# One level of Strassen's scheme in the gate and up product of an encoder's MLP

## The chip, the cores and the metric

The kernel runs on one core of one Trainium2 chip. The metric is the device time of one execution in microseconds (us). The engines that matter are TensorE (PE in the rows; its weight loads are listed as PEld), VectorE (DVE), ScalarE (ACT), GpSimd (POOL), and SyncE (SP), whose queue issues nearly all DMA transfers.

## The reference

Two encoder layers run over 1024 tokens of width 1024. Each has a mixer (attention of one kind or the other), a cross-attention into 256 memory tokens, and a gated MLP; every one is followed by a residual sum with the factor alpha and a LayerNorm. The change is in the MLP:

```python
def conv_ffn(x, w_in, conv_w, conv_b, w_out):
    g, u = jnp.split(x @ w_in, 2, axis=-1)          # 1024 -> 2 x 2816
    g = causal_depthwise_conv(g, conv_w, conv_b)    # width 3, along the tokens
    h = jax.nn.gelu(g.astype(f32)) * u.astype(f32)
    return h.astype(x.dtype) @ w_out                # 2816 -> 1024
```

All values are float32.

## The kernel before, in words

Every float32 operand of a product is split in two: a rounded part `hi` (a cast on ScalarE) and a rest `lo` (a subtraction on VectorE); `split` does both. A product is then three matmuls, hi·hi, hi·lo and lo·hi, summed in PSUM. Weights come by DMA into one of two staging buffers `st`, are split into two buffers of an arena `R` of 20 (8 `rb` that live throughout, 12 `rx` that live from the end of a mixer to the end of the MLP), and are fetched in a fixed order (`weights`, `w_emit`, `w_take`), two ahead. PSUM has eight banks of 128x512: four tiles `s1` of one bank and two tiles `d2` of two.

The normalised input of the MLP lies token-major in `acc` (eight tiles of 128 tokens by 1024). `to_xT` transposes a tile on TensorE (eight 128x128 transposes) and splits it into `xh` and `xl`, feature-major, eight K-blocks of 128 features by 1024 tokens.

The MLP's hidden width 2816 is cut into 22 blocks j of 128. `ffn_hidden` makes one block: the gate product and the up product, each 128 hidden units by 1024 tokens, as two halves of 512 tokens; a half is 8 K-blocks by 3 matmuls of 128x512 in `gemm_fm` (lines 144 to 146). VectorE and ScalarE then do the convolution (lines 379 to 382), the gelu (384), the product with the up branch (385) and the split of h. After each two blocks (four at the end) `ffn` multiplies h by the output weights, 8 token tiles by 2 halves by 3 matmuls for each block (lines 311 to 313), and VectorE adds the result onto `acc` (199, 201). The last group of blocks is followed tile by tile by the LayerNorm (`ln`, lines 171 to 181).

`mem` is the cross-attention, head by head (h = 0 to 3). In its last head the eight token tiles pass in turn through scores (`score`), a transpose of the weights (`tr`) and the product with the values (`pv`); the sum onto `acc` and LayerNorm follow, and `to_xT` transposes tile t-4 behind tile t. The last tiles' transposes are queued in `xtq` and done inside the first `ffn_hidden`.

The order of the work on each engine is laid out ahead of time by a scheduler that follows the program's order and fills in what is ready; on the chip each engine takes its list in order.

## Time and profile before

| what | us |
|---|---|
| median of 3 runs | 2884.42 |
| lowest and highest of them | 2881.32, 2886.17 |
| the profiled execution, its own time | 2884.2 |
| span of the profiled execution, first to last instruction | 2882.5 |
| mean granted TensorE clock in it | 0.998 |

The page gives busy time by engine and by line, and the windows, the timeline and the groups by form are answers of the same trace. A matmul's duration runs from when it enters the array to when its last column has left, and the next one enters before that; so the distance of two starts, not the duration, is what one more matmul adds. Waits are put down to the releaser that came last.

### The profile page before, as it was taken

To read this page: it belongs to the slowest core of one execution; us is meant where nothing else is said; L and a number is where in the kernel's file an instruction comes from. 1 tells how busy PE (TensorE), PEld (TensorE's weight loads), DVE (VectorE), ACT (ScalarE), POOL (GpSimd) and SP (SyncE) were. 2 spreads that over 40 slices of the span, in tenths; PEclk is the share of its full clock that TensorE was granted. 3 is DMA by queue.
4 is the path that set the end of the run, shared out by engine and by line. 5 is a ranking of instruction groups with operands and counts; after the bars stand their busy time and mean duration, and the time that the engine had idled before them with its cause. 6 is when DMAs were issued, how large, how long until landed. Compare 5 with 4: busy or idle time off the path is not lost.

```text
span 2882.5 us, 37533 instructions
## 1 busy us (share of the span) xinstructions
PE 2839.5 (99%) x15080; PEld 2391.4 (83%) x15080; DVE 1612.4 (56%) x2846; ACT 951.8 (33%) x1859; POOL 103.7 (4%) x155
## 2 busy tenths in 40 slices
PE   8999999999999999999999999999999999999998
PEld 7878888899988888888888777799988888888887
DVE  4647664855674444444448786665584444444446
ACT  4335463533342222222123565343343221122121
POOL 0000000100010000000001000100010000000001
PEclk9999999999999999999999999999999999999999
DMA  3113322422201111111123322332201111111111
GB/s 134 36 49 96 88 66 81 154 74 74 74 15 59 52 52 51 49 47 52 37 61 121 110 58 85 109 103 75 74 30 59 52 49 47 45 44 59 37 59 66
DMA packets 64512, 193.09 MB, mean 67 GB/s; under 512 B 11697, under 2 KB 11986, under 8 KB 64338
## 3 DMA queue, kind: packets, MB, share of 16 engines
q1 hardware_dynamic: 62976, 188.88, 21.3%
q8 instruction: 119, 1.95, 0.3%
q10 hardware_dynamic: 1362, 1.81, 0.2%
q14 instruction: 55, 0.45, 0.0%
HBM read 158.14 MB, written 9.44 MB: 58 GB/s over the span
## 4 chain that ended last, share of the span: by engine, by line
PE 75%; DVE 3%; DMA 1%; ACT 1%; issue 1%; POOL 1%; SPq 0%; DVEq 0%; ACTq 0%; POOLq 0%
PE s L145 12%; PE s L146 12%; PE s L144 12%; PE d L311 5%; PE d L313 5%; PE d L312 5%; PE s L246 2%; PE s L495 2%; PE s L497 2%; PE s L496 2%; PE d L526 2%; PE d L528 2%; PE d L527 2%; PE s L430 1%; PE s L432 1%; PE s L431 1%
## 5 line engine op out<-in xcount | busy, mean ns | idle before, releaser
L144 PE MATMUL s<-xh,rb 128*128 128x512 f32 x1824 | 714.2, 392 | 3.2 <-ACT xh L111 1.7
L145 PE MATMUL s<-xl,rb 128*128 128x512 f32 x1824 | 710.9, 390 | 0.6 <-DVE xl L112 0.6
L146 PE MATMUL s<-xh,rb 128*128 128x512 f32 x1824 | 710.5, 390 | 0.0
L112 DVE TENSOR_TENSOR rb<-st,rb 128x1024 fp32r<-128x1024 f32 (+1 forms) x207 | 252.1, 1219 | 285.9 <-ACT rb L111 278.9
L144 PEld LDWEIGHTS s<-xh,rb 128*128 128x128 f32 x1824 | 342.6, 188 | 74.1 <-ACT xh L111 2.2
L146 PEld LDWEIGHTS s<-xh,rb 128*128 128x128 f32 x1824 | 342.5, 188 | 71.2
L145 PEld LDWEIGHTS s<-xl,rb 128*128 128x128 f32 x1824 | 342.8, 188 | 69.8 <-DVE xl L112 1.5
L111 ACT CAST rb<-st 128x1024 fp32r<-128x1024 f32 (+1 forms) x207 | 217.1, 1049 | 433.3 <-PE s L145 275.2
L199 DVE TENSOR_TENSOR acc<-acc,d 128x1024 f32<-128x1024 f32 x160 | 195.3, 1221 | 198.0 <-PE d L313 167.9
L313 PE MATMUL d<-rx,rx 128*128 128x512 f32 x572 | 222.5, 389 | 0.0
L312 PE MATMUL d<-rx,rx 128*128 128x512 f32 x572 | 222.5, 389 | 0.0
L311 PE MATMUL d<-rx,rx 128*128 128x512 f32 x572 | 222.5, 389 | 0.0
L385 DVE TENSOR_TENSOR fc<-fc,s 128x512 f32<-128x512 f32 x88 | 60.5, 687 | 201.8 <-PE s L146 201.8
L111 ACT CAST rx<-st 128x1024 fp32r<-128x1024 f32 x40 | 40.5, 1051 | 339.3 <-PE d L312 321.6
L495 PE MATMUL s<-rx,xh 128*128 128x256 f32 x512 | 144.6, 282 | 0.0
L497 PE MATMUL s<-rx,xl 128*128 128x256 f32 x512 | 143.5, 280 | 0.0
L496 PE MATMUL s<-rx,xh 128*128 128x256 f32 x512 | 143.4, 280 | 0.0
L384 ACT ACTIVATE fc<-fc,cw 128x512 f32<-128x512 f32 x88 | 63.7, 724 | 225.8 <-DVE fc L382 225.8
L246 PE MATMUL s<-xh,rb 128*128 128x512 f32 x448 | 128.1, 397 | 3.7 <-ACT xh L111 1.0
L312 PEld LDWEIGHTS d<-rx,rx 128*128 128x128 f32 x572 | 107.4, 188 | 22.7
L311 PEld LDWEIGHTS d<-rx,rx 128*128 128x128 f32 x572 | 107.4, 188 | 22.3
L313 PEld LDWEIGHTS d<-rx,rx 128*128 128x128 f32 x572 | 107.4, 188 | 22.2
(300 smaller groups left out, 4952.5 us busy)
## 6 DMA issues: line engine op xcount, KB each, us to landing
st<-in_ffn_in_dram SPq DMA_DIRECT2D x88, 512.0 KB, 3.7
st<-in_ffn_out_dram SPq DMA_DIRECT2D x44, 512.0 KB, 3.6
st<-in_mem_kv_dram SPq DMA_DIRECT2D x32, 512.0 KB, 4.1
st<-in_memT_dram SPq DMA_DIRECT2D x16, 512.0 KB, 3.7
st<-in_mem_qT_dram SPq DMA_DIRECT2D x16, 512.0 KB, 3.6
st<-in_mem_out_dram SPq DMA_DIRECT2D x16, 512.0 KB, 3.6
Q<-rr SPq DMA_DIRECT2D x128, 64.0 KB, 2.0
st<-in_e_v_dram SPq DMA_DIRECT2D x8, 512.0 KB, 4.2
```

The costliest lines, as they stand in the source:

```text
L111: s.nc.scalar.copy(out=hi, in_=src)
L112: s.nc.vector.tensor_tensor(out=lo, in0=src, in1=hi.bitcast(F32), op=ALU.subtract)
L144: nc.tensor.matmul(ps, h[:, k, :], s.xh[:, k, t0:t1], start=k == 0, stop=False)
L145: nc.tensor.matmul(ps, h[:, k, :], s.xl[:, k, t0:t1], start=False, stop=False)
L146: nc.tensor.matmul(ps, l[:, k, :], s.xh[:, k, t0:t1], start=False, stop=k == NK - 1)
L199: s.nc.vector.tensor_tensor(out=a, in0=a, in1=ps, op=ALU.add)
L311: nc.tensor.matmul(o, hh[:, sl], wh[:, c], start=q == 0, stop=False)
L312: nc.tensor.matmul(o, hh[:, sl], wl[:, c], start=False, stop=False)
L313: nc.tensor.matmul(o, hl[:, sl], wh[:, c], start=False, stop=q == n - 1)
L495: nc.tensor.matmul(o, s.xh[:, k, sl], gh, start=k == 0, stop=False)
L496: nc.tensor.matmul(o, s.xh[:, k, sl], gl, start=False, stop=False)
L497: nc.tensor.matmul(o, s.xl[:, k, sl], gh, start=False, stop=k == NK - 1)
```

## The change

The gate and up product of block j is taken as a 2x2 by 2x2 block product: A11 and A12 are the gate weights for the first and second four K-blocks, A21 and A22 those of the up branch; B11, B12 are the first four K-blocks of x for the first and the last 512 tokens, B21 and B22 the second four. It is done with seven block products (Winograd's form of Strassen's scheme) in place of eight, each of four K-blocks by three matmuls of 128x512. The sums of weights S1 to S4 are made on VectorE for each j (`prep`) and split; the sums of inputs T1 to T4 are made once for each layer (`pair`, which takes token tiles t and t+4 together) and split. The first four tiles go to B11 and B21 as they come (`early`). Products that share a sum accumulate in one PSUM bank; the others are combined on VectorE (`post`). `early` and `pair` replace `to_xT` before the MLP; four products of blocks 0 and 1 that need only B11 and B21 stand between the pairs.

h is written to DRAM (`hid`), and the output product is a phase of its own: for each half of the tokens (g) and each j, h and the output weights are read back and split (`out_prep`), and four token tiles accumulate in all eight PSUM banks over the 22 blocks. `acc` serves as scratch in the meantime; x is kept in DRAM (`xres`). `mem`'s matrix G gets four buffers of its own (`GU`), and the arena keeps 16. The MLP's weights leave the list of `weights`; the next mixer's first weight is held back until the MLP's end (`hold`). The scratch that the program sets aside for DMA descriptors goes from 2048 to 1024. Lines that are left out of the diff below are pools, views and names.

```diff
+        s.hold = False
+        s.xres = s.dr.tile([T, D], F32, name="xres")
+        s.hid = [s.dr.tile([P, T], F32, name=f"hid{j}") for j in range(s.FF)]
...
-            if key[0] in ("eo", "oo") or (len(s.R.base) if key[0] in ("ok", "ov", "oa", "ob") else s.R.n()) < 2:
+            if key[0] in ("eo", "oo") or s.hold and key[0] == "ok" or (len(s.R.base) if key[0] in ("ok", "ov", "oa", "ob") else s.R.n()) < 2:
...
+        s.GU = [p.tile([P, Arena.W], F32R, name=f"gu{i}") for i in range(4)]
+        s.tmp = [p.tile([P, 512], F32, name=f"tmp{i}") for i in range(2)]
+        s.F = [p.tile([P, T + 8 + 104 * (i == 2)], F32, name=f"f{i}")[:, 0:T + 8] for i in range(3)]
+        s.open_x()
...
+    def open_x(s, more=()):
+        s.xs = ExitStack()
+        p = s.xs.enter_context(s.tc.tile_pool(name="restx", bufs=1, reuse_waits="tile"))
+        s.R.open([p.tile([P, Arena.W], F32R, name=f"rx{i}") for i in range(8)] + list(more))
+    def close_x(s):
+        s.R.close()
+        s.xs.close()
...
+    PRODS = {"P1": ("A11", "B11", 0), "P2": ("A12", "B21", 0), "P3": ("S4", "B22", 2), "P4": ("A22", "T4", 3),
+             "P5": ("S1", "T1", 2), "P6": ("S2", "T2", 1), "P7": ("S3", "T3", 1)}
...
+    def open_a(s):
+        s.xs = ExitStack()
+        p = s.xs.enter_context(s.tc.tile_pool(name="ffa", bufs=1, reuse_waits="tile"))
+        s.TB = {n: [tuple(p.tile([P, 4, 512], F32R, name=f"{n}{w}") for w in "hl")] for n in ("B11", "B21")}
+        s.p1x = [p.tile([P, 512], F32, name=f"p1x{i}") for i in range(2)]
+        for i, n in enumerate(("T2", "T3", "T4", "B22")):
+            s.TB[n] = [tuple(x[:, 2 * i:2 * i + 2, :].rearrange("p a (b t) -> p (a b) t", b=2) for x in (s.xh, s.xl))]
+        u = [t[:, 0:T].rearrange("p (k t) -> p k t", k=2) for t in s.GU]
+        s.TB["T1"] = [(u[0], u[2]), (u[1], u[3])]
...
+    def early(s, t):
+        c = slice(t * P, t * P + P)
+        s.tb_put("B11", c, s.tr4(t, 0))
+        s.tb_put("B21", c, s.tr4(t, 1))
+    def pair(s, t):
+        nc = s.nc
+        c = slice(t * P, t * P + P)
+        v = lambda a: a.rearrange("p (k c) -> p k c", k=4)
+        b11, b12, b22 = s.tr4(t, 0), s.tr4(t + 4, 0), s.tr4(t + 4, 1)
+        r11, r22, t1 = v(s.fc()), v(s.fc()), v(s.fc())
+        nc.scalar.copy(out=r11, in_=b11)
+        nc.scalar.copy(out=r22, in_=b22)
+        b21 = s.tr4(t, 1)
+        nc.vector.tensor_tensor(out=t1, in0=b12, in1=r11, op=ALU.subtract)
+        s.tb_put("T1", c, t1)
+        nc.vector.scalar_tensor_tensor(out=r11, in0=b12, scalar=-1.0, in1=r22, op0=ALU.mult, op1=ALU.add)
+        s.tb_put("T3", c, r11)
+        s.tb_put("B22", c, b22)
+        nc.vector.tensor_tensor(out=t1, in0=r22, in1=t1, op=ALU.subtract)
+        s.tb_put("T2", c, t1)
+        nc.vector.tensor_tensor(out=r22, in0=b21, in1=t1, op=ALU.subtract)
+        s.tb_put("T4", c, r22)
...
+        slot = lambda i, n=1: accf[:, 512 * i:512 * (i + n)]
+        raws = [s.stg.tile([P, T], F32, name="st", tag="st") for _ in range(2)]
+        P1s, P5s, U2s = [slot(0), slot(1)], [slot(2), slot(3)], [slot(4), slot(5)]
+        tmps = [s.tmp, [slot(6), slot(7)]]
+        hs = [slot(8, 2), slot(10, 2)]
+        order = ["P1", "P5", "P6", "P2", "P3", "P7", "P4"]
+        seq = [(0, "P1"), (0, "P2"), (1, "P1"), (1, "P2")]
+        for j in range(FF):
+            seq += [(j, b) for b in order if (j, b) not in seq]
+        raw, blk, X, loc = {}, {}, {}, {}
...
+        def load(j, up):
+            r = raws[2 * (j % 2) + up]
+            nc.sync.dma_start(out=r, in_=s.I["ffn_in"][l, j + FF * up])
+            a = "A%d" % (up + 1)
+            raw.setdefault(j, {}).update({a + "1": r[:, 0:512], a + "2": r[:, 512:T]})
...
+        def prep(j, b):
+            n = s.PRODS[b][0]
+            r = raw[j]
+            a, c = tmps[j % 2]
+            tt = lambda o, x, y, op: nc.vector.tensor_tensor(out=o, in0=x, in1=y, op=op)
+            if n == "S1":
+                tt(a, r["A21"], r["A22"], ALU.add)
+                r[n] = a
+            elif n == "S2":
+                tt(c, r["S1"], r["A11"], ALU.subtract)
+                r[n] = c
+            elif n == "S4":
+                tt(a, r["A12"], r["S2"], ALU.subtract)
+                r[n] = a
+            elif n == "S3":
+                tt(c, r["A11"], r["A21"], ALU.subtract)
+                r[n] = c
+            u = s.R.get(True)
+            s.split(u[:, 0:512], u[:, 512:T], r[n])
+            blk[j, b] = u
+            if b == "P4" and j + 2 < FF:
+                load(j + 2, 0)
+                load(j + 2, 1)
+        def prod(j, b):
+            _, n, i = s.PRODS[b]
+            if b == "P1":
+                d = s.d2()
+                X[j] = {0: d[:, 0:512], 2: d[:, 512:1024]}
+            if i not in X[j]:
+                X[j][i] = s.s1()
+            o = X[j][i]
+            u = blk.pop((j, b))
+            h, lo = (u[:, w:w + 512].rearrange("p (k c) -> p k c", k=4) for w in (0, 512))
+            k = 0
+            first = b in ("P1", "P4", "P5", "P6")
+            for bh, bl in s.TB[n]:
+                for q in range(bh.shape[1]):
+                    z = dict(skip_group_check=True)
+                    nc.tensor.matmul(o, h[:, k, :], bh[:, q, :], start=first and k == 0, stop=False, **z)
+                    nc.tensor.matmul(o, h[:, k, :], bl[:, q, :], start=False, stop=False, **z)
+                    nc.tensor.matmul(o, lo[:, k, :], bh[:, q, :], start=False, stop=k == 3, **z)
+                    k += 1
+            s.R.put(u)
...
+        def tap(j, hf):
+            g, o = gs[j % 2], 512 * hf
+            c = s.fc()
+            loc[j, "c", hf] = c
+            nc.scalar.activation(out=c, in_=g[:, o + 2:o + 514], func=AF.Copy, scale=cw[:, j, 2:3])
+            for i in (1, 0):
+                nc.vector.scalar_tensor_tensor(out=c, in0=g[:, o + i:o + i + 512], scalar=cw[:, j, i:i + 1], in1=c,
+                                               op0=ALU.mult, op1=ALU.add)
+        def gelu(j, hf):
+            c = loc[j, "c", hf]
+            nc.scalar.activation(out=c, in_=c, func=AF.Gelu_apprx_tanh, bias=cw[:, j, 3:4])
+        def post(j, b):
+            x, q = X[j], j % 2
+            g, u2, p5 = gs[q], U2s[q], P5s[q]
+            add = lambda o, a, c: nc.vector.tensor_tensor(out=o, in0=a, in1=c, op=ALU.add)
+            if b == "P1":
+                loc[j, "p1"] = s.p1x[q] if j < 2 else P1s[q]
+                nc.scalar.copy(out=loc[j, "p1"], in_=x[0])
+                return
+            p1 = loc[j, "p1"]
+            if b == "P5":
+                nc.scalar.copy(out=p5, in_=x[2])
+            elif b == "P6":
+                add(u2, x[1], p1)
+            elif b == "P2":
+                nc.scalar.copy(out=g[:, 2:514], in_=x[0])
+            elif b == "P3":
+                add(g[:, 514:1026], x[2], u2)
+                tap(j, 0)
+            elif b == "P7":
+                add(p1, x[1], p1)
+                gelu(j, 0)
+                tap(j, 1)
+                add(p5, p1, p5)
+            else:
+                add(u2, x[3], p1)
+                gelu(j, 1)
+                h = hs[q]
+                for hf, y in ((0, u2), (1, p5)):
+                    nc.vector.tensor_tensor(out=h[:, 512 * hf:512 * hf + 512], in0=loc.pop((j, "c", hf)), in1=y,
+                                            op=ALU.mult)
+                nc.sync.dma_start(out=s.hid[j], in_=h)
+                del X[j], raw[j]
...
+        def ahead(i):
+            nonlocal n
+            while n < len(seq) and n <= i and len(s.R.base):
+                if seq[n] in ((1, "P1"), (1, "P5")):
+                    load(1, seq[n][1] == "P5")
+                prep(*seq[n])
+                n += 1
+        ahead(1)
+        yield
+        gs = s.F[0:2]
+        raws += [s.F[2][:, 0:T], slot(14, 2)]
+        for t in gs:
+            nc.gpsimd.memset(t[:, 0:2], 0.0)
+        for i, (j, b) in enumerate(seq):
+            ahead(i)
+            prod(j, b)
+            post(j, b)
+            ahead(min(i + 6, 8) if i < 4 else i + 6)
+            if i in (1, 3):
+                yield
+            if j == FF - 1 and b == "P2":
+                s.xs.close()
+                s.open_x(s.GU)
+                s.out_start(l)
+            elif j == FF - 1 and b in ("P3", "P7", "P4"):
+                s.out_prep(("P3", "P7", "P4").index(b))
...
+    def out_prep(s, upto):
+        nc = s.nc
+        while s.bn < len(s.bseq) and s.bn <= upto and s.R.n() >= 3:
+            g, j = s.bseq[s.bn]
+            s.bn += 1
+            st = s.stg.tile([P, T], F32, name="st", tag="st")
+            nc.sync.dma_start(out=st, in_=s.I["ffn_out%d" % s.bl][j * P:(j + 1) * P, :])
+            c = s.fc()
+            nc.sync.dma_start(out=c, in_=s.hid[j][:, 512 * g:512 * g + 512])
+            w, lo, u = s.R.get(), s.R.get(), s.R.get()
+            s.split(u[:, 0:512], u[:, 512:T], c)
+            s.split(w, lo, st)
+            s.bu[g, j] = (w, lo, u)
...
+        s.lag = None
+        for g in range(2):
+            ps = [s.d2(), s.d2(), [s.s1(), s.s1()], [s.s1(), s.s1()]]
+            for j in range(FF - (L if g else 0)):
+                s.out_prep(g * FF + j)
+                for i in range(4):
+                    mm(4 * g + i, ps[i], [j])
+                s.R.put(*s.bu.pop((g, j)))
+                s.out_prep(g * FF + j + 4)
+                if 2 <= g * FF + j < 10:
+                    t = g * FF + j - 2
+                    nc.sync.dma_start(out=s.acc[:, t, :], in_=s.xres[t * P:(t + 1) * P, :])
+                if late and j >= 1:
+                    t, tot = late.pop(0)
+                    s.ln(t, tot)
+                    done(t)
+            if g == 0:
+                for t in range(4):
+                    tot = s.tot()
+                    s.evac(t, ps[t], tot)
+                    late.append((t, tot))
+        s.out_prep(2 * FF)
+        s.hold = False
+        xq = list(range(6))
+        for i in range(4):
+            t = 4 + i
+            mm(t, ps[i], range(FF - L, FF))
+            if i == 3:
+                for j in range(FF - L, FF):
+                    s.R.put(*s.bu.pop((1, j)))
+            s.w_emit()
+            tot = s.tot()
+            if out is not None:
+                s.last_tile(t, ps[i], tot, out)
+                continue
+            s.evac(t, ps[i], tot)
+            s.ln(t, tot)
+            done(t)
+            for _ in range(2 * i):
+                if xq and xq[0] < t - 1:
+                    s.to_xT(xq.pop(0), s.d2())
...
-            g = [R.get(shift=True) for _ in range(4)]
+            g = [u[:, Arena.SHIFT:Arena.SHIFT + T] for u in s.GU]
...
+                R.put(*pts)
+                pts = [R.get(True), R.get(True)]
+                s.close_x()
+                s.open_a()
+                f = s.ffn_gen(l)
+                next(f)
...
-                    s.to_xT(t - 4)
+                    s.early(t - 4)
...
-                s.to_xT(4)
+                s.pair(0)
...
+        s.pair(1)
+        next(f)
+        s.pair(2)
+        next(f)
+        s.pair(3)
+        for _ in f:
+            pass
...
-        i, prev = 0, []
-        for nb in Net.FBLK + [0]:
-            for j in range(i, i + nb):
-                r += [(("fi", l, j), I["ffn_in"][l, j]), (("fi", l, j + Net.FF), I["ffn_in"][l, j + Net.FF])]
-            r += [(("fo", l, j), rows("ffn_out%d" % l, j)) for j in prev]
-            prev = list(range(i, i + nb))
-            i += nb
```

## Rows read from the trace of the kernel before

**Rows 1.** The page's head: span, and busy time by engine.

```profile
span 2882.5 us, 37533 instructions
...
PE 2839.5 (99%) x15080; PEld 2391.4 (83%) x15080; DVE 1612.4 (56%) x2846; ACT 951.8 (33%) x1859; POOL 103.7 (4%) x155
```

**Rows 2.** Windows, us from span start: busy time per engine, granted clock, DMA share, GB/s.

```profile
800.00:821.00 21.00, 21.00 (x137) 18.53 (x136) 19.21 (x40) 10.77 (x24) 4.34 (x3) 1.00 0.00 1
...
821.00:845.00 24.00, 22.84 (x116) 18.88 (x115) 17.97 (x28) 9.70 (x16) 4.59 (x6) 1.00 0.00 1
...
867.00:1482.00 615.00, 615.00 (x2715) 509.21 (x2714) 277.96 (x323) 132.15 (x178) 1.69 (x17) 1.00 0.16 50
...
2150.00:2172.00 22.00, 20.84 (x103) 17.05 (x103) 15.79 (x26) 8.62 (x14) 3.14 (x5) 1.00 0.00 1
```

**Rows 3.** Line 144's instructions in layer 0's MLP: count, min/median/max ns, first and last start.

```profile
L144 PE MATMUL s<-xh,rb x704: 389/389/499, 824.6 to 1481.1; 128*128 128x512 f32 x176
```

**Rows 4.** Timeline of TensorE, steady stretch: start us, duration us, instruction.

```profile
1099.82 0.39 PE L145 MATMUL s<-xl,rb 128*128 128x512 f32 x1
...
1109.79 0.39 PE L144 MATMUL s<-xh,rb 128*128 128x512 f32 x1
```

**Rows 5.** Timeline of TensorE where tile 4 is transposed, end of layer 0's cross-attention.

```profile
820.95 1.03 PE L192 MATMUL s<-ident,acc 128*128 128x128 f32 x8
...
821.74 0.48 PE L526 MATMUL d<-rx,rx 128*128 128x512 f32 x1
...
822.06 0.39 PE L527 MATMUL d<-rx,rx 128*128 128x512 f32 x1
```

**Rows 6.** VectorE's groups by form: busy us, mean ns, idle before.

```profile
L382 DVE SCALAR_TENSOR_TENSOR fc<-f,cw,fc 128x512 f32<-128x512 f32 x88 | 66.2, 752 | 3.1
...
L112 DVE TENSOR_TENSOR rx<-fc,rx 128x512 fp32r<-128x512 f32 x88 | 60.6, 688 | 27.4 <-ACT rx L111 27.4
...
L385 DVE TENSOR_TENSOR fc<-fc,s 128x512 f32<-128x512 f32 x88 | 60.5, 687 | 201.8 <-PE s L146 201.8
```

**Rows 7.** ScalarE's groups by form, the same columns.

```profile
L384 ACT ACTIVATE fc<-fc,cw 128x512 f32<-128x512 f32 x88 | 63.7, 724 | 225.8 <-DVE fc L382 225.8
...
L111 ACT CAST rx<-fc 128x512 fp32r<-128x512 f32 x88 | 54.2, 616 | 50.8 <-DVE fc L385 50.8
...
L372 ACT COPY f<-s 128x512 f32<-128x512 f32 x88 | 51.3, 583 | 207.2 <-PE s L146 207.2
```

**Rows 8.** Timeline of VectorE from cross-attention into layer 0's MLP.

```profile
820.10 0.42 DVE L112 TENSOR_TENSOR rx<-s,rx 128x256 fp32r<-128x256 f32 x1
...
822.22 1.22 DVE L201 SCALAR_TENSOR_TENSOR acc<-acc,d 128x1024 f32<-128x1024 f32 x1
...
831.74 1.28 DVE L181 SCALAR_TENSOR_TENSOR acc<-acc,lnrs,f 128x1024 f32<-128x1024 f32 x1
...
832.94 1.28 DVE L112 TENSOR_TENSOR xl<-s,xh 128x512 fp32r<-128x512 f32 x2
...
834.14 0.75 DVE L380 SCALAR_TENSOR_TENSOR fc<-f,cw,fc 128x512 f32<-128x512 f32 x1
...
834.92 0.75 DVE L382 SCALAR_TENSOR_TENSOR fc<-f,cw,fc 128x512 f32<-128x512 f32 x1
```

**Rows 9.** Timeline of TensorE after a stall in layer 1's attention.

```profile
1742.84 0.39 PE L727 MATMUL d<-khd,Q 128*128 128x256 f32 x1 [2.05 <-ACT p L741]
...
1745.97 0.41 PE L727 MATMUL d<-khd,Q 128*128 128x256 f32 x1
...
1746.18 0.41 PE L728 MATMUL d<-kl,Q 128*128 128x256 f32 x1
```

**Rows 10.** Windows, the same stretch: the granted clock is the column behind POOL.

```profile
1744.00:1746.00 2.00, 1.92 (x10) 1.52 (x9) 1.12 (x6) 1.97 (x8) 0.00 (x0) 0.50 0.40 100
```

**Rows 11.** The page's DMA issues: one row, us from issue to landing.

```profile
st<-in_ffn_in_dram SPq DMA_DIRECT2D x88, 512.0 KB, 3.7
```

**Rows 12.** The page's GB/s over forty equal slices of the span.

```profile
GB/s 134 36 49 96 88 66 81 154 74 74 74 15 59 52 52 51 49 47 52 37 61 121 110 58 85 109 103 75 74 30 59 52 49 47 45 44 59 37 59 66
```

More of the change, by code (lines that the diff above doesn't have):

```diff
@@ L121, in w_emit @@
             s.nc.sync.dma_start(out=st, in_=src)
-            h, l = (s.R.get(key[0] != "fo", key[0] in ("mT", "ev")) for _ in range(2))
+            own = key[0] == "mo" and key[2] >= 6
+            h, l = (s.R.get(not own, key[0] in ("mT", "ev")) for _ in range(2))
             s.split(h, l, st)
@@ new lines, in evac @@
+    def evac(s, t, ps, tot):
+        if not isinstance(ps, list):
+            return s.acc_add(t, ps, True, tot)
+        tt = s.tiny("tt", 2)
+        for hf in range(2):
+            c = slice(hf * 512, hf * 512 + 512)
+            s.nc.vector.scalar_tensor_tensor(out=s.acc[:, t, c], in0=s.acc[:, t, c], scalar=ALPHA, in1=ps[hf],
+                                             op0=ALU.mult, op1=ALU.add, accum_out=tt[:, hf:hf + 1])
+        s.nc.vector.tensor_tensor(out=tot, in0=tt[:, 0:1], in1=tt[:, 1:2], op=ALU.add)
@@ L470, in VW @@
             vt = st["v", h]
-            w = [R.get() for _ in range(4)]
+            w = [R.get(h == 3) for _ in range(4)]
             st["W", h] = w
@@ L532, in pv @@
                 s.ln(t, tot)
+                nc.sync.dma_start(out=s.xres[t * P:(t + 1) * P, :], in_=s.acc[:, t, :])
         for _ in kv(0):
```

163 lines of the change are left out of this document (54 added, 109 removed).

## The prediction

> **What bounds the kernel now.** I read the busy times first. TensorE is busy for 2839.5 of 2882.5 us, VectorE for 56 per cent, ScalarE for 33 [rows 1]. Busy time alone would not show that TensorE is the bound in the MLP, so the windows come next: over 615 us of layer 0's MLP, TensorE has no idle time at all, VectorE works 278 us and ScalarE 132, at full granted clock [rows 2]. The MLP costs what its matmuls cost, and fewer of them is time saved, as long as nothing else comes late. The windows also show the tight place: at the end of the cross-attention VectorE is busy 19.2 of 21.0 us with TensorE still full, and in the step into the MLP TensorE idles for 1.16 us in either layer (22.84 of 24.00 and 20.84 of 22.00) [rows 2].
>
> What one matmul costs is not its 389 ns duration [rows 3]. On the timeline 44 matmuls lie between 1099.82 and 1109.79, 0.2266 us from start to start [rows 4]. Eight transposes fill 820.95 to about 821.83 (the second matmul behind them starts at 822.06, the first one distance earlier), so 0.11 us each [rows 5].
>
> **The products.** One of three lines has 704 matmuls in a layer's gate and up product [rows 3], so 2112 for a layer and 4224 for both, which is 22 x 2 x 2 x 8 x 3 x 2. After it a block takes 7 products x 4 K-blocks x 3 = 84 instead of 96. 12 x 44 = 528 matmuls fall away, at 0.2266 us: 119.7 us. Operand shapes are as before, so I keep the distance. The output product keeps its number of matmuls.
>
> **Blocks in the steady state.** TensorE needs 84 x 0.2266 = 19.0 us for a block. VectorE has 22 operations of 128x512 for it: 4 weight sums, 7 split rests, 5 combinations, 2 products with the up branch, and 4 convolution steps. A pair of split rests lies 1.20 us apart (832.94 to 834.14), 0.60 each; a convolution step 0.78 (834.14 to 834.92) [rows 8]. So 18 x 0.60 + 4 x 0.78 = 13.9 us; by full durations of 0.69 and 0.75 [rows 6] it is 15.4. ScalarE has 7 casts at 0.62, 3 copies at 0.58, 2 scaled copies, which no row shows and which I put at the cast's 0.62, and 2 gelus at 0.72 [rows 7], 8.8 us. Both fit beside 19.0, and weights are prepared up to six products (16 us) ahead. PSUM banks are taken again two blocks later; P2 and P3 accumulate onto banks that ScalarE has to read first, each with at least two products (5.4 us) in between, except in the first two blocks. I cost this at nothing; the cover is VectorE's 3.6 to 5.1 us of slack per block, and without it every microsecond per block costs 44.
>
> **The step into the MLP.** This is the cost that I expect. P5 needs T1 of all 512 token pairs, thus all eight LayerNorms and the fourth `pair`. Only pv(7) and four products can run before it: 12 + 48 matmuls, 13.6 us. Count from 820.95, where tile 4's transposes start now. VectorE becomes free at about 820.5, behind the split that starts at 820.10 [rows 8]. Then its list is:
> - the LayerNorms of tiles 5 to 7 and the sums of tiles 6 and 7: six passes at 1.20 (831.74 to 832.94), two at 1.22 [rows 8], and short ones, 10.0 us;
> - three pairs: each has four sums at 0.60 and five split rests at 0.60 (T1's in two pieces), 5.6 us with the slightly longer pieces, 16.8 together; of the fourth pair the part up to T1, 1.3;
> - weights for the next seven products, which stand ahead of the fourth pair in the program: 7 rests and 4 sums, of which 12 x 0.60 = 7.2 us I count (one more for a longer sum).
>
> That is 35.3 us, so 855.8. Handovers between casts and rests leave holes: the 88 rests of h waited 27.4 us, 0.31 each [rows 6]. With some 13 of these in the pairs I add 4 us, and P5 starts at 860. From 820.95 that is 39 us, less 13.6 of work that was there anyhow, less what the step costs now, 32 transposes (3.5) and 1.2 us idle: 20.7 more. The 32 additional transposes of a layer lie inside it. Behind P5, P6 waits for T2, and after holes the clock may be low for a few us: when TensorE had idled for 2.05 us, before 1742.84, a 256-column matmul every 0.21 us followed, as at 1745.97 and 1746.18 [rows 9], and the granted clock was 0.50, which is the 1.2 GHz level [rows 10]. A stretch of some 4 us at that level loses 2. The step costs 22.7 us more in each layer, 45.4 in both.
>
> Its bounds: if VectorE has no holes and takes the last weights (4.8 us of the list) later, P5 starts at 851 and the step costs 11.8. If no cast is hidden, ScalarE's 4.3 us for each pair (7 passes) add 17 us, P5 starts at 877, and the step costs 40 with the clock. Both layers: 24 to 80 around 45. I take the middle because VectorE filled 19.2 of 21 us in the window before, with the same mixture of casts and rests [rows 2].
>
> The Trainium skill, page "TensorE: Matmul & The Clock Gate", Part 1, says that the engine's default is the low clock and that only sustained activity releases it. By that the gappy step would run low from end to end; the rows above agree that a gap brings the level down and show the return.
>
> **The output phase and the small edits.** A step of it is 24 matmuls, 5.4 us, and needs 768 KB (weights 512, h 256), 145 GB/s; the highest slice now moves 154 [rows 12], and 512 KB land in 3.7 us [rows 11]. With two staging buffers a load has two steps, 10.9 us, for landing (3.7), cast and rest (2.4 by twice the 512-column rows [rows 6, 7]). The first load comes after P2 of the last block, three products (8.2 us) ahead of its use. In eight steps `acc` is loaded as well, on the same SP queue; no transfer waits there for anything late, since h has been computed. VectorE has 1.8 of 5.4 us. Evacuating four tiles between halves takes 1.22 us each [rows 8] while TensorE works on the others (1.36 us each). All that: nothing; with a cover gone, each of two starts loses at most one landing, 4 us. SP's `xres` and `hid` stores queue behind LayerNorm and h; the load of block j+2 is issued ahead of h of block j, and has a block's 19 us. The hold on the next mixer's weight, the missing `memset`s on GpSimd, G's own buffers, the smaller arena and the descriptor scratch: nothing, since TensorE has no waits for these in [rows 2]. The end of the kernel is the same last tile.
>
> **The sum.** 2884.2 - 119.7 + 45.4 = 2809.9 us, against the profiled execution's own time; the median of the runs, 2884.42, is the same within 0.2 us. Forecast 2810.
>
> **Rivals.**
> - *VectorE becomes the bound in the blocks* (slower). Its operations alternate with ScalarE's in order. If no handover is hidden, a block's 15.4 us grow by 7 casts (4.3) and by two scaled copies and gelus (2.7) to 22.4; 3.4 more than TensorE's 19.0, 44 times: 148 us, 2958. It decides the sign from a period of 20.7 us (74 us saved by 44 blocks). For it: the rests of h do wait 0.31 each [rows 6]. Against: that is VectorE without other work; the window before shows it 91 per cent busy under a full TensorE [rows 2], and six products of lead. Half of it (19.7 us) would give 2839.
> - *The two halves of a `d2` tile are ordered as one.* Then P5 waits for the copy of P1, and P3 for that of P2, in each block: 0.58 [rows 7] and the 0.16 by which a matmul's duration exceeds its distance [rows 3, 4], 0.74 to 0.85 with a handover, 88 times: 65 to 75 us, 2875 to 2885, about no change. No row shows halves used in that way; they are separate banks, so I think it unlikely.
> - *The step runs at 1.2 GHz throughout.* TensorE's 13.6 us and 64 transposes (7.0) take 41, P5 and P6 lose 5.4: the step costs 28 and the time is 2821. The rows show what follows a hole of 2 us, not a whole step, so it is a smaller chance. The Trainium skill's section named above would make this the likely case.
>
> **How the numbers follow.** Forecast 0.74 (2788 to 2845, the step's bounds); low clock throughout 0.10; VectorE half exposed 0.06 (2839, up to 2860); fully exposed 0.06 (2958); halves as one 0.04. The range 2784 to 2850 takes in the step's bounds with one late start on either side, and leaves out some 0.15. A measurement of this kernel can tell 0.2 per cent, 5.8 us, from no change. Faster 0.92, same 0.02 (half of the last case), slower 0.06.
>
> **What would show it.** Right: 84 matmuls for a block at 0.227 us, TensorE without idle time over twenty blocks and in the output phase, a hole of 10 to 20 us in TensorE between the four early products and P5, ended by VectorE's rests of T1. Wrong: waits of TensorE on ScalarE's copies or on split weights in each block; a VectorE busy for over 19 us of a block; waits on DMA in the output phase; a step whose hole is a few us only.

## The result, and the profile after

The changed kernel takes 2816.35 us, the median of 4 runs (2808.83 to 2818.53); the kernel before took 2884.14 beside it. The ratio is 0.9761, with a 95 per cent interval of 0.9741 to 0.9781: faster by 2.4 per cent. The forecast was 2810, with a range of 2784 to 2850. The profiled execution has 2815.04 us of its own and a span of 2813.2.

The head of the page after, to be read against [rows 1]:

```profile
span 2813.2 us, 38138 instructions
...
PE 2752.1 (98%) x14616; PEld 2298.0 (82%) x14616; DVE 1815.0 (65%) x3359; ACT 1185.6 (42%) x2303; POOL 105.4 (4%) x115
```

The span is 69.3 us shorter. The trace lists 464 matmuls fewer, the 528 less the 64 additional transposes. At the prediction's 119.7 us for the 528, 50.4 us were paid for them. Where they were paid is read from four instants that both traces have: the start of tile 4's transposes in either layer (820.95 and 2147.79 before, 822.63 and 2115.75 after), the first product of the second layer's mixer (1552.37 and 1517.02), and the end (2882.5 and 2813.2). Each MLP should have lost 59.85 us of matmuls.

| stretch | before | after | lost |
|---|---|---|---|
| start to tile 4, layer 0 | 820.95 | 822.63 | 1.7 |
| tile 4 to the second mixer | 731.4 | 694.4 | 22.8 |
| second mixer to tile 4, layer 1 | 595.4 | 598.7 | 3.3 |
| tile 4, layer 1, to the end | 734.7 | 697.45 | 22.6 |

Windows of the kernel after, the same columns as [rows 2] (start and end, length, then busy us and count for PE, PEld, DVE, ACT, POOL, then granted clock, DMA share, GB/s): the step into the MLP, twenty blocks, the output phase.

```profile
830.00:840.00 10.00, 5.85 (x31) 3.93 (x29) 10.00 (x19) 7.50 (x15) 2.15 (x3) 0.93 0.17 61
840.00:850.00 10.00, 7.65 (x26) 5.66 (x27) 10.00 (x19) 6.38 (x14) 0.00 (x0) 0.56 0.58 201
850.00:860.00 10.00, 7.74 (x38) 5.93 (x38) 8.67 (x17) 6.44 (x13) 0.00 (x0) 1.00 0.32 108
870.00:1270.00 400.00, 400.00 (x1742) 323.45 (x1741) 294.63 (x456) 173.95 (x289) 0.00 (x0) 1.00 0.26 88
1270.00:1500.00 230.00, 230.00 (x1016) 189.89 (x1014) 106.53 (x132) 77.17 (x101) 10.52 (x5) 1.00 0.54 175
```

The step has TensorE busy for 21.2 of 30 us while VectorE is busy for 28.7; in the blocks and in the output phase TensorE shows no idle time at all. Yet the blocks hide a loss: 1742 matmuls in 400 us are 0.2296 us each, not the 0.2266 of [rows 4]. The first product of block 2 starts at 885.11 and that of block 21 at 1252.41, 19.33 us for each block where the prediction had 19.04; in layer 1 it is 19.32. On the timeline of TensorE inside a block the difference has a place:

```profile
907.85 0.39 PE L419 MATMUL s<-xh,rb 128*128 128x512 f32 x1
908.08 0.39 PE L420 MATMUL s<-xl,rb 128*128 128x512 f32 x1
908.30 0.50 PE L419 MATMUL d<-gu,rb 128*128 128x512 f32 x1
908.64 0.40 PE L420 MATMUL d<-gu,rb 128*128 128x512 f32 x1
908.88 0.40 PE L421 MATMUL d<-gu,rb 128*128 128x512 f32 x1
```

Five matmuls of P6 (`s<-xh`) run ahead of P5 (`d<-gu`), and the first of P5 keeps the next one 0.34 us away instead of 0.23. The waits of the same window say what P5 and P3 stood behind, the copies of P1 (line 444) and P2 (line 452), 20 times each in twenty blocks (us in all, times, longest):

```profile
PEld d L419 <- ACT acc L444: 5.1, 20, 0.3
PEld d L419 <- ACT f L452: 5.1, 20, 0.3
```

In the step itself, TensorE first (a product of block 1, half of it at half speed, then P5), then SP's load of block 1's gate weights into LayerNorm's buffer, then ScalarE in front of P5:

```profile
846.55 0.79 PE L419 MATMUL d<-B11h,rb 128*128 128x512 f32 x1 [0.48 <-ACT rb L114]
847.57 0.63 PE L421 MATMUL d<-B11h,rb 128*128 128x512 f32 x1
847.99 0.63 PE L419 MATMUL d<-B11h,rb 128*128 128x512 f32 x1
...
856.85 0.50 PE L419 MATMUL d<-gu,rb 128*128 128x512 f32 x1 [1.92 <-ACT gu L114]
```

```profile
841.63 0.43 SPq L376 DMA_DIRECT2D f<-in_ffn_in_dram  x1
```

```profile
854.41 0.59 ACT L452 COPY f<-d 128x512 f32<-128x512 f32 x1 [2.07 <-PE d L421]
854.89 0.59 ACT L344 COPY fc<-s 128x512 f32<-128x512 f32 x1
855.37 0.60 ACT L114 CAST xh<-s 128x512 fp32r<-128x512 f32 x1
855.85 0.64 ACT L114 CAST xh<-fc 128x512 fp32r<-128x512 f32 x1
856.37 0.73 ACT L114 CAST gu<-fc 128x256 fp32r<-128x256 f32 x2
```

P5 starts 34.2 us behind tile 4's transposes, and in layer 1 33.5 (2149.24 against 2115.75). Last, the start of the second mixer on VectorE and on TensorE. The kernel before had only the wait of 1.5 us there:

```profile
PE s L144 <- DVE xl L112: 1.5, 1, 1.5
```

The kernel after also waits for the two rotary tables:

```profile
1526.64 0.68 DVE L889 TENSOR_TENSOR fc<-s,cos 64x512 f32<-64x512 f32 x1 [2.68 <-DMA cos<-tab]
...
1530.65 0.69 DVE L890 TENSOR_TENSOR fc<-s,sin 64x512 f32<-64x512 f32 x1 [2.73 <-DMA sin<-tab]
```

```profile
1532.82 0.66 PE L196 MATMUL s<-ident,acc 128*128 128x128 f32 x4 [2.74 <-DVE fc L892]
1534.98 0.79 PE L148 MATMUL s<-xh,rb 128*128 128x512 f32 x1 [1.50 <-DVE xl L115]
1535.57 0.63 PE L149 MATMUL s<-xl,rb 128*128 128x512 f32 x1
1536.00 0.63 PE L150 MATMUL s<-xh,rb 128*128 128x512 f32 x1
```

### The profile page after: what moved, and what is told of

Read it like the earlier page. It is cut to its first block, busy times and chain, and to the rows that moved or that the text cites. A ratio compares the mean times of both kernels' runs of the same rounds, so it can differ in the third digit from the quotient of the medians.

```text
span 2813.2 us, 38138 instructions
## 1 busy us (share of the span) xinstructions
PE 2752.1 (98%) x14616; PEld 2298.0 (82%) x14616; DVE 1815.0 (65%) x3359; ACT 1185.6 (42%) x2303; POOL 105.4 (4%) x115
## 3 DMA queue, kind: packets, MB, share of 16 engines
q1 hardware_dynamic: 92928, 274.87, 30.3%
## 4 chain that ended last, share of the span: by engine, by line
PE 73%; DVE 5%; ACT 1%; DMA 1%; issue 1%; POOL 0%; SPq 0%; DVEq 0%; ACTq 0%; POOLq 0%
PE d L419 6%; PE d L420 6%; PE d L421 6%; PE s L419 4%; PE s L421 4%; PE s L420 4%; PE s L551 3%; PE s L552 3%; PE s L553 3%; PE d L552 3%; PE d L551 3%; PE d L553 3%; PE s L261 2%; PE s L712 2%; PE s L714 2%; PE s L713 2%
## 5 line engine op out<-in xcount | busy, mean ns | idle before, releaser
L115 DVE TENSOR_TENSOR rb<-st,rb 128x1024 fp32r<-128x1024 f32 (+2 forms) x179 | 181.9, 1017 | 113.2 <-ACT rb L114 107.1
L114 ACT CAST rb<-st 128x1024 fp32r<-128x1024 f32 (+2 forms) x179 | 158.9, 888 | 209.3 <-issue 84.4
L419 PE MATMUL s<-xh,rb 128*128 128x512 f32 x528 | 205.4, 389 | 0.0
L421 PE MATMUL s<-xh,rb 128*128 128x512 f32 x528 | 205.4, 389 | 0.0
L420 PE MATMUL s<-xl,rb 128*128 128x512 f32 x528 | 205.3, 389 | 0.0
L148 PE MATMUL s<-xh,rb 128*128 128x512 f32 x416 | 166.9, 401 | 1.5 <-DVE xl L115 1.5
L149 PE MATMUL s<-xl,rb 128*128 128x512 f32 x416 | 163.6, 393 | 0.0
L150 PE MATMUL s<-xh,rb 128*128 128x512 f32 x416 | 163.2, 392 | 0.0
L431 DVE SCALAR_TENSOR_TENSOR fc<-f,cw,fc 128x512 f32<-128x512 f32 x176 | 131.7, 748 | 29.6 <-ACT fc L429 28.3
L712 PE MATMUL s<-gu,xh 128*128 128x256 f32 x512 | 144.6, 282 | 0.0
L714 PE MATMUL s<-gu,xl 128*128 128x256 f32 x512 | 143.5, 280 | 0.0
L115 DVE TENSOR_TENSOR rb<-acc,rb 128x512 fp32r<-128x512 f32 (+1 forms) x124 | 92.6, 748 | 78.8 <-ACT rb L114 78.4
L713 PE MATMUL s<-gu,xh 128*128 128x256 f32 x512 | 143.4, 280 | 0.0
L261 PE MATMUL s<-xh,rb 128*128 128x512 f32 x448 | 128.1, 397 | 3.5 <-ACT xh L114 1.1
L421 PEld LDWEIGHTS s<-xh,rb 128*128 128x128 f32 x528 | 99.1, 188 | 20.8
L419 PEld LDWEIGHTS s<-xh,rb 128*128 128x128 f32 x528 | 99.1, 188 | 20.6
L420 PEld LDWEIGHTS s<-xl,rb 128*128 128x128 f32 x528 | 99.1, 188 | 20.5
L115 DVE TENSOR_TENSOR rx<-st,rx 128x1024 fp32r<-128x1024 f32 x70 | 85.7, 1225 | 30.6 <-ACT rx L114 30.4
```

The source lines that it names most:

```text
L114: s.nc.scalar.copy(out=hi, in_=src)
L115: s.nc.vector.tensor_tensor(out=lo, in0=src, in1=hi.bitcast(F32), op=ALU.subtract)
L261: nc.tensor.matmul(ps[hf], a[:, c], b[:, hf * 512:hf * 512 + 512], start=st, stop=sp)
L419: nc.tensor.matmul(o, h[:, k, :], bh[:, q, :], start=first and k == 0, stop=False, **z)
L420: nc.tensor.matmul(o, h[:, k, :], bl[:, q, :], start=False, stop=False, **z)
L421: nc.tensor.matmul(o, lo[:, k, :], bh[:, q, :], start=False, stop=k == 3, **z)
```

## The experiments

Theory after the comparison: TensorE bounds the blocks, the 0.29 us per block come from the two halves of one `d2` tile being ordered as one, and the step is set by VectorE's list. The rivals: any start of a product costs that much; the step is set by something else that ends at about the same time. All ratios are to the kernel before, on the same chip, with a 95 per cent interval. "Step" is the time from the first early product (P1 of block 0) to P5, and to P1 of block 2, in layer 0 and layer 1.

| kernel | ratio | median us | to P5 | to block 2 | a block |
|---|---|---|---|---|---|
| after | 0.9761 [0.9741, 0.9781] | 2816.35 | 29.7, 29.0 | 58.0, 58.5 | 19.33 |
| again | 0.9761 [0.9746, 0.9775] | 2812.24 | 30.4, 30.4 | 58.7, 58.6 | 19.29 |
| halves | 0.9721 [0.9702, 0.9740] | 2801.76 | 30.5, 30.1 | 58.7, 58.4 | 19.04 |
| dummy | 0.9840 [0.9821, 0.9859] | 2835.58 | 41.4, 41.9 | 70.4, 71.2 | 19.34 |
| twice | 1.0183 [1.0168, 1.0198] | 2935.28 | 29.7, 30.3 | 63.4, 64.1 | 22.05 |
| late | 0.9754 [0.9740, 0.9767] | 2811.94 | 29.8, 30.1 | 58.5, 58.7 | 19.36 |
| pool | 0.9788 [0.9774, 0.9801] | 2822.11 | 36.7, 35.5 | 64.4, 63.2 | 19.34 |
| comb | 0.9760 [0.9746, 0.9773] | 2814.64 | 36.9, 36.1 | 64.8, 64.0 | 19.04 |
| tabs | 0.9756 [0.9742, 0.9770] | 2811.72 | 30.7, 30.3 | 60.2, 58.5 | 19.34 |
| tile0 | 0.9755 [0.9742, 0.9768] | 2811.75 | 28.9, 28.9 | 58.8, 58.1 | 19.30 |
| gate | 0.9784 [0.9771, 0.9798] | 2821.01 | 29.8, 30.3 | 58.1, 58.6 | 19.34 |
| best | 0.9746 [0.9733, 0.9760] | 2809.10 | 28.9, 28.9 | 57.8, 57.8 | 19.04 |
| trio | 0.9702 [0.9689, 0.9715] | 2798.05 | 27.2, 27.1 | 56.3, 56.7 | 19.04 |

The first two lines are one kernel: between its executions P5 moves by up to 1.4 us, so the columns of the step tell nothing finer than that.

**again**, the changed kernel once more, as the measure for the others.

> The changed kernel as it is, to stand beside the others on one chip. All theories: 2816 us within 0.2 per cent; a block of the MLP every 19.3 us from P1 to P1, the fourth pair's T1 ready about 34 us behind tile 4's transposes.

As expected.

**halves**: which products share a two-bank tile.

```diff
-                X[j] = {0: d[:, 0:512], 2: d[:, 512:1024]}
+                X[j] = {0: d[:, 0:512], 3: d[:, 512:1024]}
```

> Only the PSUM banks are dealt otherwise: the two-bank tile holds P1 and P2 in one half and P4 in the other, P5 and P3 get a bank of their own. Theory (the halves of a tile are ordered as one, and TensorE's list pays for each switch that the scheduler makes around it): no matmul waits for the copy of P1 or of P2 any more, a block takes 84 x 0.2266 = 19.04 us instead of 19.31, and 44 blocks give 12 us back: about 2804. Rival (the 0.28 us belong to the start of any product, whichever bank it writes): blocks stay at 19.3 us, 2816 within 3 us. Second rival (P3 and P7 now compete for the four single banks): blocks of over 19.4 us, 2822 or more.

The window of the blocks, to be set beside the one of after:

```profile
870.00:1270.00 400.00, 400.00 (x1765) 331.02 (x1764) 300.78 (x460) 180.37 (x292) 0.00 (x0) 1.00 0.27 93
```

23 more matmuls fit into the same 400 us; both lines of waits on lines 444 and 452 are gone, and a block takes 19.04 us, as the prediction had it. 44 blocks by 0.25 to 0.29 are 11 to 13 us, and the ratio falls by 0.0040, 11.5 us. So P5 and P3 did wait for the copies of the other half of their tile, and both rivals of this run's expectation fall. The busy share of TensorE is the same 400.00 of 400 in both.

**twice**: P4's twelve matmuls are done twice, so that the up branch is not that of the MLP.

```diff
-            for bh, bl in s.TB[n]:
+            for bh, bl in s.TB[n] * (2 if b == "P4" else 1):
+                first = first and k < 4
+                k = k % 4
```

> The twelve matmuls of P4 are issued twice in every block, so that TensorE does eight products in a block and the upper product is not that of the MLP; everything else is as in the changed kernel. Theory (TensorE bounds the blocks, so a product costs its matmuls): a block takes 19.31 + 12 x 0.2266 = 22.03 us, and 44 blocks add 119.6 us: 2936. Rival (VectorE and ScalarE with their handovers hold a part of the block): less than 110 us added, and a TensorE with idle time in the blocks of the changed kernel that the twelve matmuls fill.

The block grows by 2.76 us and the time by 0.0422 of the kernel before, 122 us, against 119.6 by the distance of [rows 4]. A product that is added costs its twelve matmuls, within 2 per cent: TensorE bounds the blocks, and the term of 119.7 us is confirmed from the other side. With eight products the scheme takes 1.8 per cent longer than the kernel before.

**dummy**: four VectorE subtractions more for each pair of tiles.

```diff
         s.tb_put("T4", c, r22)
+        for _ in range(4):
+            nc.vector.tensor_tensor(out=t1, in0=r22, in1=t1, op=ALU.subtract)
```

> Four VectorE subtractions of 128x512 are added behind each of the four pairs of tiles, 0.6 us each. Twelve of them lie ahead of T1 of the fourth pair. Theory (VectorE's list sets the start of P5): P5 starts 12 x 0.60 = 7.2 us later in each layer and the four behind the last pair delay P6 or the first combinations by up to 2.4 us: 14 to 19 us in all, 2830 to 2835. Rival (the handovers between casts, transposes and rests set it, and VectorE has room between them): 0 to 3 us for each layer, 2816 to 2822.

P5 comes 11.0 and 11.5 us later, and the time is 23 us longer: more than the theory's 14 to 19. On the timeline of TensorE the hole in front of P5 is now a single one, and it ends with the cast of the last T1:

```profile
868.15 0.80 PE L421 MATMUL d<-gu,rb 128*128 128x512 f32 x1 [10.22 <-ACT gu L114]
```

VectorE works through its list up to there. Besides the twelve additional operations (7.2 us) the scheduler had put six more weight operations (3.6 us) ahead of the last T1's rest: nine rests and six sums, where the changed kernel has seven and two. That makes 10.8 us, and the idle time between (2.2 and 2.7 us, 2.5 in again) is as before. So P5 came later by what the list had grown by: a longer list does set it.

**late**: five weight operations are to leave the list.

```diff
-            ahead(min(i + 6, 8) if i < 4 else i + 6)
+            ahead(min(i + 2, 5) if i < 4 else i + 6)
```

> In the step into the MLP the sums and rests for P3, P7 and P4 of block 0 are placed behind the products that precede them, not ahead of the last pair of tiles: 5 VectorE operations, 3.0 us by 0.60 each, leave the list that ends with the last T1. Theory (VectorE's list sets the start of P5): P5 starts up to 3.0 us earlier in each layer, 2 to 6 us in all, ratio to the kernel before 0.9740 to 0.9755. Rival (the hand-overs of casts and transposes set it, or the operations only move behind T1 and delay P6 and P3 instead): the changed kernel's 0.9761 within 0.0007.

The step stays where it was, within what one kernel shows, and the ratio is at the border of the two ranges. But the list that ran is hardly shorter. Up to the last T1's rest (`gu<-fc,gu`) VectorE still does both sums and six of the seven rests, in either layer; the scheduler moved only the rest for P4 (`rb<-st,rb`) behind it. First the two lines of after, then those of late:

```profile
851.50 0.68 DVE L115 TENSOR_TENSOR rb<-st,rb 128x512 fp32r<-128x512 f32 x1
...
857.21 0.75 DVE L115 TENSOR_TENSOR gu<-fc,gu 128x256 fp32r<-128x256 f32 x2
```

```profile
856.13 0.75 DVE L115 TENSOR_TENSOR gu<-fc,gu 128x256 fp32r<-128x256 f32 x2
...
858.00 0.69 DVE L115 TENSOR_TENSOR rb<-st,rb 128x512 fp32r<-128x512 f32 x1
```

One operation is 0.6 us, less than the step moves from run to run. This run tells nothing of what a shorter list would give; trio does.

**tile0**: what the lines of the step suggest as the second chain. The gate weights of block 1 wait for LayerNorm's buffer (841.63), land 4.0 us later, their product runs at half speed, and the copy behind the next product (854.41) stands in ScalarE's queue ahead of the last pair's casts.

```diff
-            r = raws[2 * (j % 2) + up]
+            r = slot(0, 2) if j == 1 and not up else raws[2 * (j % 2) + up]
```

> One load of each MLP goes elsewhere: the gate weights of block 1 are loaded into the first token tile of the scratch, which is free once the first pair's transposes have read it (about 826 us in the trace), instead of into LayerNorm's gain buffer, which is free only after the last LayerNorm pass (838.3). Theory (the late part of the step is set by the two early products of block 1: buffer free at 838.3, load 4.1, cast, first product at 843.7 and half of it at half clock, second product until 852.0, and behind its copy ScalarE's casts of the last T1): these products move into TensorE's idle time between 833 and 843, P5 starts 3 to 5 us earlier in each layer, 6 to 10 us in all, ratio 0.9727 to 0.9740. Rival (VectorE's list of 35 us sets P5 by itself): P5 moves by less than 1 us in each layer, ratio 0.9750 to 0.9765. Second rival (the products, now queued on TensorE ahead of the pairs' transposes, hold these up): slower than the changed kernel, 0.977 or more.

The two products of block 1 move: the last matmul of P1 starts at 837.84 instead of 850.27. But P5 starts only 0.1 to 1.5 us earlier than in the two traces of the changed kernel, and it starts at half clock:

```profile
846.97 1.12 PE L327 MATMUL s<-ident,acc 128*128 128x128 f32 x4 [3.21 <-ACT fc L343]
...
854.16 0.80 PE L419 MATMUL d<-gu,rb 128*128 128x512 f32 x1 [3.28 <-ACT gu L114]
```

The idle time has moved from before these products to behind them; 850 to 860 us now has a granted clock of 0.52 where it was 1.00, and block 2 starts when it did. The first rival holds: VectorE is full from 830 to 860 (29.8 of 30 us). What the second chain had cost is VectorE's idle time up to the last T1's rest, 1.1 to 2.5 us in the changed kernel and 0.8 here, in either layer.

**pool**: the sums and rests of the first nine weights go to GpSimd.

```diff
-        def prep(j, b):
+        def prep(j, b, e=None):
+            e = e or nc.vector
...
-                prep(*seq[n])
+                prep(*seq[n], nc.gpsimd if n < 9 else None)
```

> The sums and the rests of the first nine prepared weights of each layer are made by GpSimd instead of VectorE: 13 operations of 128x512, of which about 12, 7.2 us by 0.60 each, lie in the list ahead of the last T1. Theory (VectorE's list sets the start of P5, and GpSimd, busy for 4 per cent of the span, has room): 6 us less for each layer, 12 in all, ratio 0.972. Rival (GpSimd is slower at such an operation, and the first products, or LayerNorm's own operation on GpSimd, come late behind it): 0.976 or more, with TensorE waiting for a GpSimd rest and VectorE for GpSimd.

Slower by 8 us, 5 to 6 in either step. GpSimd's operation takes 1.3 us and two rests 3.49, where VectorE needs 0.60 for one, and a LayerNorm pass on VectorE, which waited for GpSimd's own part of LayerNorm, took 2.28 us instead of 1.28:

```profile
825.84 1.29 POOL L385 TENSOR_TENSOR tmp<-st,tmp 128x512 f32<-128x512 f32 x1
...
831.16 3.49 POOL L400 TENSOR_TENSOR rb<-tmp,rb 128x512 fp32r<-128x512 f32 x2
```

```profile
831.23 2.28 DVE L185 SCALAR_TENSOR_TENSOR acc<-acc,lnrs,f 128x1024 f32<-128x1024 f32 x1 [2.41 <-POOL lnrs L164]
```

Both engines were slow in the same stretch, and VectorE, rid of seven rests, was idle for 7.1 and 5.9 us ahead of the last T1's rest. The Trainium skill, page "SBUF — State Buffer", section "SBUF: two separate sides", says that VectorE operations with two inputs from SBUF and GpSimd operations that read SBUF share a pair of ports under an exclusive lock; the two lengthened operations agree with that, and no run here separates it from other causes.

**comb**: halves and pool together.

> The bank assignment in which P1 shares its two-bank tile with P4, together with the first nine weights prepared on GpSimd. If both act as separate terms: 11 us for the banks (0.9721) and 12 for GpSimd, ratio 0.968. If GpSimd is the slower engine there: 0.972 or more.

Blocks of 19.04 us and a step of 36.9 and 36.1: the two terms add within the intervals, one gain and one loss.

**tabs** and **gate**: the loads beside the rotary tables at the start of the second mixer. For tabs, the second pair of query weights was held back in the program until the first key half:

```diff
-            if key[0] in ("eo", "oo") or s.hold and key[0] == "ok" or (len
+            if key[0] in ("eo", "oo") or s.hold and key[0] == "ok" or key == ("oa", 1) and not s.early_oa or (len
...
             k_half(uk, 0)
+            s.early_oa = True
+            s.w_emit()
```

> At the boundary of the layers the second pair of query weights (two loads of 512 KB) is held back until the first key half has been issued, so that the two rotary tables do not share the DMA engines with them. Theory (the 3 to 4 us that the odd mixer's start lost come from these loads): VectorE waits for the tables less than 1.5 us instead of 4.6 (3.50 + 1.09), TensorE's 1.91 us of idle time ahead of the transposes goes, and with the matmuls at half clock behind it 2 to 4 us are saved: ratio 0.9747 to 0.9755. Rival (the tables are late because of where their loads are issued, or the x that is stored at the same time is what they share with): the waits stay over 3 us, 0.9761 within 0.0005.

The loads were issued where they had been (1516.54 and 1518.40, against 1515.72 and 1517.58 in again): nothing on the chip made them wait, and the scheduler placed them as soon as their buffers were free. This run tells nothing of the theory. For gate the edit of tabs was kept, and each load got a true dependence on its table:

```diff
+            if key in (("oa", 1), ("ob", 1)):
+                s.nc.vector.tensor_copy(out=st[:, 0:1], in_=s.tabt[key[0] == "ob"][:, 0:1])
             s.nc.sync.dma_start(out=st, in_=src)
```

> At the boundary of the layers the second pair of query weights (two loads of 512 KB) now really comes later: VectorE copies one column of the cosine or sine table into the staging buffer first, so that each load waits until its table has landed. Theory (these two loads take the DMA engines' time from the tables): the waits of VectorE for the tables fall from 4.6 us to under 2.5, TensorE's 1.9 us of idle time goes, 2 to 4 us in all, ratio 0.9747 to 0.9755. Rival (the tables share with the store of x and with their own small packets, or are issued late): the waits stay over 3.5 us, and the time is the changed kernel's 0.9761 within 0.0006; it could be slower by 2 us if the query weights come late.

The table loads' rows of DMA issues over the start of the second mixer (KB each, median us from issue to landing), of the kernel before, of again and of gate:

```profile
cos<-tab ACTq DMA_DIRECT2D x1, 512.0 KB, 5.0
sin<-tab ACTq DMA_DIRECT2D x1, 512.0 KB, 5.9
```

```profile
cos<-tab ACTq DMA_DIRECT2D x1, 512.0 KB, 7.2
sin<-tab ACTq DMA_DIRECT2D x1, 512.0 KB, 9.3
```

```profile
cos<-tab ACTq DMA_DIRECT2D x1, 512.0 KB, 3.2
sin<-tab ACTq DMA_DIRECT2D x1, 512.0 KB, 4.2
```

VectorE's waits for the tables (3.5 and 1.1 us in again) and TensorE's 1.9 us are gone, so the transfers under way beside the tables were the cause. They were beside them in the kernel before too, but later: its second load was issued 5.5 us behind the mixer's first product (1557.86 and 1552.37), that of after 3.6 (1520.62 and 1517.02), and the tables landed in time. But gate is 7 us slower. SP has issued 32 small transfers for the queries, among others, by the time it comes to the second weight, and TensorE waits later:

```profile
1541.63 14.25 SPq L859 DMA_DIRECT2D Q<-rr  x16
1566.37 13.50 SPq L859 DMA_DIRECT2D Q<-rr  x16
1579.91 0.58 SPq L127 DMA_DIRECT2D st<-in_o_b_dram  x1
```

```profile
1578.06 0.38 PE L958 MATMUL d<-khd,Q 128*128 128x256 f32 x1 [3.39 <-ACT p L972]
1580.66 0.58 PE L958 MATMUL d<-khd,Q 128*128 128x256 f32 x1 [1.01 <-ACT acc L972]
1584.29 0.58 PE L958 MATMUL d<-khd,Q 128*128 128x256 f32 x1 [1.98 <-ACT acc L972]
```

Whether these waits come from the late weight or from the order around it was not separated.

**best**: halves, tile0 and gate together.

> The bank assignment of P1 with P4, block 1's gate weights in the first token tile, and the held-back query weights, together. If the terms add: 11 us for the banks, 6 to 10 for the early load, 2 to 4 for the tables, so 19 to 25 under the changed kernel, ratio 0.967 to 0.9695. If only the banks act: 0.9721.

2809.10 us, 0.9746 [0.9733, 0.9760]: the banks' gain less gate's loss, and not the sum expected.

**trio**: halves, tile0 and late together. Here the scheduler did move work: VectorE does one sum and five rests ahead of the last T1's rest, three operations fewer than in the changed kernel.

> The bank assignment of P1 with P4, block 1's gate weights loaded early into the first token tile, and the weights of P3, P7 and P4 of block 0 left to VectorE behind the last pair. Taken alone, the second moved P5 by 1.5 us and the third by 0.5, since another of three chains ended almost as late: VectorE's list, the two early products of block 1, ScalarE's order. Theory (these end together, so only taking two away at once pays): P5 starts 29 us or less behind the first early product less another 2 to 4, that is after 25 to 27 us instead of 30.4, and the time is 5 to 9 us under that of the bank assignment alone (0.9721): ratio 0.969 to 0.9705. Rival (ScalarE's casts or the low clock behind TensorE's hole take it back): P5 earlier by less than 2 us, or the next blocks later by as much, ratio 0.9712 to 0.973.

P5 starts at 27.2 and 27.1 us, earlier than in any other kernel, and block 2 2.0 to 2.3 us earlier than in again, in both layers: 4.3 us together, short of the 5 to 9 expected, though the ratio lies in the range expected. P5 gains about 3.2 us, a third of which is given back behind it. The two parts add: best, which has tile0 but the whole list, starts P5 at 28.9, and three operations of 0.60 less make 27.1. That both must go at once to pay is not shown. The ratio, 0.9702, is 0.0059 under the changed kernel's, of which the banks have 0.0040; its interval overlaps that of halves alone, so the step's part rests on the two traces. With 2798 us it is the fastest kernel here.

## Why the prediction was right, and where it was not

The sign and the place of the main cost were right, its size was too large by a quarter, and the total was 6 us off. That it was so near is in good part luck: the step came out 12.5 us cheaper than its two terms, the blocks 12.5 dearer than nothing, and the starts 5.0. Two things that the prediction had named as signs of being wrong were seen: waits on ScalarE's copies in each block, and a step without a long hole.

| term | predicted | measured |
|---|---|---|
| 528 matmuls | -119.7 | -119.7, not measured alone |
| step up to P5, both layers | 41.4 | 31.1 |
| low clock and the rest of the step | 4 | 1.8, what is left over |
| blocks | 0 | 12.5 |
| start of the second mixer and of the kernel | 0 | 5.0 |
| sum | -74.3 | -69.3 |

- *The products.* Right, as far as shown: twice prices twelve matmuls at 2.76 us in place, by the predicted 2.72.
- *The step up to P5.* Too dear by 5 us in each layer. From tile 4's transposes, less 13.6 and 4.7 as in the prediction: 15.9 and 15.2 us, not 20.7. VectorE was free at 822.2 and came to the last T1 at 857.2, 35.0 us against a list of 35.3; but nine of the twelve weight operations stood in it, and of the 4 us of holes under 2: between 830 and 850 VectorE was busy for 20 of 20 us, with LayerNorm passes and weights between the casts. The expected hole of 10 to 20 us in one piece was wrong: TensorE idles 8.8 us between 830 and 860, in pieces of at most 1.9.
- *What sets the step.* "Ended by VectorE's rests of T1" holds. Added up on the timelines from VectorE's first free moment (822.2 in after) to the start of the last T1's rest, VectorE's work is 33.2 us in after and again, 44.2 in dummy, 32.7 in late, 33.1 in tile0 and 31.3 in trio, in either layer; its idle time is 1.1 to 2.5 us, 2.2 to 2.7, 2.3 to 2.5, 0.8 and 0.8. In all of them P5 starts within 0.4 us of that rest. The idle time is where the second chain, the two products of block 1, comes in: tile0 takes away 0.3 to 1.7 us of it. The prediction counted these two as work that could run before P5, and missed that their weights are loaded into a buffer that LayerNorm holds until its last pass.
- *The low clock.* The prediction expected some 4 us of it behind P5 in each layer. The granted clock was 0.93, 0.56 and 1.00 in the three windows from 830 to 860, 0.83 over all 30 us, which makes some 10 us at the 1.2 GHz level. All of that lay ahead of P5, inside the step's term. In layer 1 the clock fell a second time around P5: 0.84, 0.50 and 0.80 in the windows of 2 us from 2148 to 2154. The rival of a step at 1.2 GHz throughout falls, since two thirds of the 30 us lay at the upper level. The Trainium skill, page "TensorE: Matmul & The Clock Gate", Part 1, has the low clock as the default; the trace agrees for the stretch behind the waits of 838 to 846, and not for the step as a whole.
- *The blocks, costed at nothing.* This is the term that failed: 0.29 us by 22 blocks in layer 0 and 0.28 by 22 in layer 1, against the 19.04 of halves. VectorE's slack was there (295 of 400 us busy against 13.9 of 19.0 predicted, 74 and 73 per cent), so the rival of VectorE as the bound falls. (That rival's "half of it", 19.7 us, is the casts alone, 15.4 and 4.3, and not half of the 7 us of handovers; nothing hung on it.) What cost was the rival called unlikely, the halves of a `d2` tile ordered as one, and halves shows it. Its price was wrong too: 0.74 to 0.85 us for each wait assumed that TensorE stands still, but the scheduler had put five matmuls of the next product into the gap, and 0.14 us were left of each. "No row shows halves used in that way" is a reason for a larger chance than 0.04.
- *The output phase.* Right: 230.00 of 230 us busy, 0.2264 us for a matmul, with 175 GB/s.
- *The hold on the next mixer's weight and the other small edits, put at nothing.* Wrong by 3.3 us at the second mixer, where the tables came late beside the second pair of query weights, as gate shows. Which of the edits made the second of these loads 1.9 us earlier than before, counted from the mixer's first product, was not tested. The 1.7 us ahead of the first MLP stay open; the same kernel differs by as much from run to run there (tile 4 and what follows it lie 2.9 us earlier in again).

## What to carry to other kernels

An engine that shows no idle time can still lose: count its instructions in a long window and compare their distance with that of an undisturbed stretch, since 0.29 us in a block are invisible in a busy share of 100 per cent. Accumulators that are read at different times belong into different tiles, however separate their banks are. An edit of the program's order is not yet an edit of the list that runs: late was to move five operations and moved one, tabs moved no load, and dummy brought six operations more than its edit says. So count what the list held in either trace before the time is read: counted in that way, adding (dummy) and taking away (trio) both came out at their length.

## What was not expected of the hardware

GpSimd's 128x512 operation took 1.3 us against 0.60 from start to start on VectorE, and beside it a VectorE pass over 1024 columns took 2.28 us instead of 1.28. Of four transfers of 512 KB, issued within 2 us by two engines at the start of the second mixer, the first took 3.6 us from issue to landing and the other three 7.2 to 9.3 (again); with the weights held back the two tables took 3.2 and 4.2 (gate). The first matmul behind a wait for another engine kept its successor 0.34 us away, instead of 0.23, though TensorE was never listed as idle in the blocks.
